# Compressing products after the whole fourth projection, and weight sums behind the last chunk's addition

## The chip, the cores and the metric

The kernel runs on one core of one Trainium2 chip. The metric is the device time of one execution in microseconds (us); the time before is the median of three runs, 2373.29 us.

## The reference, cut to what matters

Two layers of a decoder trunk run on one sequence of 512 tokens and 1024 features. Each layer has a gated feed-forward block, a mixing block and a second feed-forward block; the mixing block has three attention branches, one of which reads compressed keys and values.

```python
for l in range(DEPTH):                                     # DEPTH = 2
    h = rms_norm(x, ffn1_norm[l])
    x = x + 0.5 * swiglu(h, ffn1_w_gate[l], ffn1_w_up[l], ffn1_w_down[l])
    h = rms_norm(x, mix_norm[l])
    (nq, nkc, nvc, nks, nvs, nkw, nvw, ngate, sq, sk, sv, wq, wk, wv, bgate) = jnp.split(h @ w_in[l], SPLIT_POINTS, axis=-1)
    y_nsa = nsa_attention(...)             # compressed, selected and window branch
    y_sb = stick_breaking_attention(...)   # 4 heads
    y_swa = swa_sink_attention(...)
    merged = g0 * (y_nsa @ w_up_nsa[l]) + g1 * (y_sb @ w_up_sb[l]) + g2 * (y_swa @ w_up_swa[l])
    x = x + merged @ w_out[l]
    h = rms_norm(x, ffn2_norm[l])
    x = x + 0.5 * swiglu(h, ffn2_w_gate[l], ffn2_w_up[l], ffn2_w_down[l])

def compress(t, w1, w2):                   # t: keys or values, blocks of 32 tokens, step 16
    blocks = t[:, cmp_idx] + cmp_pos[:, None, :]
    blocks = blocks.transpose(0, 3, 1, 2, 4).reshape(B, G, n_cmp, CMP_LEN * Dh)
    return jax.nn.silu(blocks @ w1) @ w2   # w1: 2048 x 256, the "compressing products" are blocks @ w1
```

## The kernel before, in words

All data are 32-bit. A product is made of three: each operand is split into a high part (a cast to fp32r on ScalarE) and a low part (the difference, on VectorE), and TensorE adds high times high, high times low and low times high (`mm3`, lines 205 to 207). A weight block is fetched by SyncE into a raw tile (`fetch`, line 173, tag `wraw`, 3 buffers) and split into `whi` and `wlo` (`split`, lines 191 and 192, 3 buffers each). Tile, the framework, plans the order of the instructions on every engine itself: it walks the traced program with a simulated clock and takes, of what is ready, what was traced first. Buffers of one tag are handed out in the order in which they are asked for. Instructions made through `fpe`, `fact`, `fdve` keep the order of the program, and `behind(ins, earlier)` adds an edge that only fixes an order.

**The mixing block's front** (`mix_front`) makes six projections of the normed input (`project`, line 672 for the products). Each projection goes over four quarters of the input features; a quarter has one weight block and, at 512 columns, 24 products of 512 columns. Between projections stand pieces of the attention work: the generator `sb` gives the stick-breaking heads one half at a time (scores at lines 763 and 764, sigmoids on ScalarE at 832 and 833, a scan on VectorE at 838, transposes and the product with the values at 780 to 795), and `more` gives gate logits (24 products each, a 512 KB weight block), which fill TensorE where it would wait. The fourth projection of the change's name is index 4 of `GROUPS`, `nkv`, counted from zero. Its argument `mid` is called after each quarter g and traces the compressing products of the chunks in `COMPRESS[g]`: before, none after quarter 0, chunks 0 and 1 after quarter 1, chunk 2 after quarter 2, chunk 3 after quarter 3. A chunk (`compress_in`, products at line 939) has two weight blocks of 512 KB, one for keys and one for values, and 32 products of 256 columns, for which each block is split first. They add up in PSUM bank 2 (`bank("c")`), which the stick-breaking scores use until then (`bank("s")`).

**The feed-forward block** takes its gate and up products in a Strassen-like form: a `Pair` has seven products of 24 matmuls of 256 columns each (`product`, line 413 in the profile for all that keeps the program's order), made of four weight blocks a11, a12, a21, a22 and sums of them. s1 is a sum of two blocks made by DMA: SyncE loads the first (line 436), GpSimd's DMA adds the second into the same tile (line 437). s2 = s1 - a11, s3 and s4 are made on VectorE (line 442). The first three products of a pair are a11 with b11 (bank X), s1 with t1 (bank W) and s2 with t2 (bank X again, after a copy of X to Y on ScalarE). b and t are forms of the input x, made by `Crossed.add` chunk by chunk as x is finished (lines 279 to 342); the last chunk (k = 7) makes t2 at once and the rest late.

At the end of a block the first pair of the next is prepared ahead (`Pair.ahead`): `before_last` is called when the products of the last of the eight output chunks are traced and before its addition to x. There are three such places: from the mixing block to the second feed-forward block in both layers (addition at line 1225), and from the second feed-forward block of layer 0 to the first of layer 1 (line 648 makes half of the product, line 652 adds it). `ahead` loads the blocks, then traces a11's high and low part, s1's high part (446) and low part (450), the sum s2 (442) and s2's high part (446). Inside a feed-forward block `ahead` is used too, between its two phases and after the opening.

Of the kernel before, what the change touches and what calls it, by code (L numbers as in the profile page):

```python
# [23 lines left out]
KD = D // P  # L24
# [32 lines left out]

COMPRESS = ((), (0, 1), (2,), (3,))

# [37 lines left out]
def trunk(ctx, tc, I, out):  # L97
# [319 lines left out]
    class Pair:  # L417
# [21 lines left out]
        def sum(self, n, dve):  # L439
            a, b, op = self.SUMS[n]  # L440
            self.v[n] = whole("u")
            dve.tensor_tensor(self.v[n], self.v[a], self.v[b], op=op)

# [4 lines left out]
        def lo(self, n, dve):  # L448
            lo = wp.tile([P, 8, P], F32R, name=nm("wlo"), tag="wlo", bufs=3).rearrange("p a b -> p (a b)")
            dve.tensor_tensor(lo, self.v[n], f32(self.parts[n][0]), op=ALU.subtract)  # L450
            self.parts[n].append(lo)

        def product(self, o, n, form, first):
# [9 lines left out]

        def ahead(self):

            self.load("a11")
            self.load_sum()
            self.load("a12", "a21", "a22")
            self.hi("a11", act)
            self.lo("a11", dve)  # L470
            self.hi("s1", act)
            self.lo("s1", dve)
            self.sum("s2", dve)
            self.hi("s2", act)

        def gate(self, i, t):
# [115 lines left out]

    def ffn(l, which, nrm, after, before_last=lambda: None):
        gu_name, d_name = f"wgu{which}", f"wd{which}"
# [6 lines left out]
        for ph, ((f0, fn), cuts) in enumerate(PHASES):  # L601
# [30 lines left out]
            for d in range(KD):  # L632
# [18 lines left out]
                else:  # L651
                    dve.tensor_tensor(x[d], x[d], e, op=ALU.add)
                    after(d)


# [441 lines left out]

    def mix(l, nrm, nxt, before_last):
        early = iter(range(EARLY))
# [14 lines left out]
        psum(acc=(3, 7, 0, 1, 2, 4, 5, 6), f=(3, 7))  # L1114
        mix_back(l, nxt.add, gls, y_ns, y_sb, y_sw, before_last)

# [75 lines left out]

    def mix_back(l, after, gls, y_ns, y_sb, y_sw, before_last):

# [22 lines left out]
        for d in range(KD):  # L1217
# [5 lines left out]
            if d == KD - 1:  # L1223
                before_last()
            dve.tensor_tensor(x[d], p, x[d], op=ALU.add)
            after(d)


# [28 lines left out]
    for l in range(L):  # L1257
# [11 lines left out]
        def start(l, which, nxt):  # L1269
            nxt.first = Pair(l, f"wgu{which}", 0, nxt)  # L1270
            nxt.first.ahead()

        mix(l, nrm, nxt, lambda: start(l, 2, nxt))
        nrm = nxt
        if l + 1 < L:
            nxt = Crossed(3 * (l + 1))
            ffn(l, 2, nrm, nxt.add, lambda: start(l + 1, 1, nxt))
            nrm = nxt
# [67 lines left out]
```

## Time and profile before

| what | value |
|---|---|
| runs | 2368.54, 2373.29, 2373.84 us; median 2373.29 |
| profiled execution | 2371.2 us, its span on the engines 2369.4 us |
| TensorE busy | 2328.6 us, 98% of the span, 14484 products |
| VectorE busy | 1693.2 us, 71% |
| ScalarE busy | 1185.8 us, 50% |
| GpSimd busy | 478.4 us, 20% |
| DMA | 289 MB, 122 GB/s over the span |

A time in the profile counts from the span's start. Matmuls overlap, so the pace of a row of them is read from start to start. PEclk is the share of TensorE's full clock that was granted: 1.00 is 2.4 GHz, 0.50 is 1.2 GHz. What stands in brackets behind an instruction is the idle time of its engine before it and what ended that.

### The profile page before, as it was taken

How to read it: one execution, taken by the hardware profiler on the slowest of the kernel's cores; microseconds unless marked ns; L12 is line 12 of the kernel's file. 1: busy time of each engine (PE TensorE's matmuls, PEld its weight loads, DVE VectorE, ACT ScalarE, POOL GpSimd, SP SyncE). 2: the span in 40 equal slices, each digit the busy share in tenths (PEclk: the TensorE clock that was granted, in tenths of full speed). 3: DMA queues.
4: the chain of work that ended last, by engine and by line, in shares of the span. 5: the costliest groups of instructions: out<-in, count | busy, mean ns of one | idle time of the engine just before them, and what ended most of it. 6: DMA issues, size and time to landing. Idle time of an engine off the chain costs nothing. (4 is left out here: it accounts for less than half of the span.)

```text
span 2369.4 us, 37950 instructions
## 1 busy us (share of the span) xinstructions
PE 2328.6 (98%) x14484; PEld 2064.2 (87%) x14484; DVE 1693.2 (71%) x2979; ACT 1185.8 (50%) x2145; POOL 478.4 (20%) x617
## 2 busy tenths in 40 slices
PE   8999999999999999999999999999999999999999
PEld 8989987877888799899899899878778878998997
DVE  8855864776677798558788568638767777984684
ACT  6533543565666555335455345435556664552351
POOL 2011011523333510110100100114233344001100
PEclk9999999999999999999999999999999999999999
DMA  6534443232323345444344444422322233544433
GB/s 205 149 123 124 137 121 114 82 130 90 101 73 120 125 143 152 121 135 136 114 137 141 135 129 124 149 87 101 118 86 95 78 122 123 144 136 131 141 114 100
DMA packets 95474, 289.24 MB, mean 122 GB/s; under 512 B 11573, under 2 KB 13410, under 8 KB 95292
## 3 DMA queue, kind: packets, MB, share of 16 engines
q1 hardware_dynamic: 89100, 264.28, 33.6%
q0 software_dynamic: 6192, 22.55, 5.6%
q8 instruction: 113, 1.85, 0.3%
q14 instruction: 69, 0.57, 0.1%
HBM read 275.70 MB, written 11.08 MB: 121 GB/s over the span
## 5 line engine op out<-in xcount | busy, mean ns | idle before, releaser
L191 ACT CAST whi<-wraw 128x1024 fp32r<-128x1024 f32 (+4 forms) x224 | 193.1, 867 | 370.4 <-PE acc L207 244.4
L192 DVE TENSOR_TENSOR wlo<-wraw,whi 128x1024 fp32r<-128x1024 f32 (+4 forms) x224 | 239.7, 1075 | 180.0 <-ACT whi L191 179.9
L413 ACT CAST whi<-u 128x1024 fp32r<-128x1024 f32 x156 | 163.9, 1050 | 248.7 <-DVE u L413 160.1
L208 PE MATMUL acc<-u,wlo 128*128 128x512 f32 x704 | 275.9, 395 | 1.1 <-DVE wlo L192 1.1
L206 PE MATMUL acc<-u,whi 128*128 128x512 f32 x704 | 276.6, 395 | 0.0
L207 PE MATMUL acc<-u,whi 128*128 128x512 f32 x704 | 276.5, 394 | 0.0
L672 PE MATMUL acc<-whi,u 128*128 128x512 f32 (+2 forms) x768 | 220.4, 363 | 0.0
L413 DVE TENSOR_TENSOR wlo<-u,whi 128x1024 fp32r<-128x1024 f32 x164 | 204.4, 1246 | 20.9 <-ACT whi L413 20.4
L437 POOL DMA_DIRECT2D u<-in_wgu x43 | 37.7, 876 | 753.4 <-DMA u<-in_wgu 389.4
L413 PE MATMUL X<-u,whi 128*128 128x256 f32 x1376 | 181.4, 284 | 5.2 <-ACT Y L413 3.5
L413 PEld LDWEIGHTS X<-u,whi 128*128 128x128 f32 x1376 | 171.6, 190 | 8.9 <-ACT Y L413 3.9
L208 PEld LDWEIGHTS acc<-u,wlo 128*128 128x128 f32 x704 | 132.2, 188 | 32.9 <-DVE wlo L192 2.0
L206 PEld LDWEIGHTS acc<-u,whi 128*128 128x128 f32 x704 | 132.4, 188 | 31.6 <-ACT whi L191 0.8
L207 PEld LDWEIGHTS acc<-u,whi 128*128 128x128 f32 x704 | 132.3, 188 | 30.7
L672 PEld LDWEIGHTS acc<-whi,u 128*128 128x128 f32 x768 | 136.3, 188 | 23.4 <-issue 1.7
L672 PE MATMUL acc<-wlo,u 128*128 128x512 f32 (+2 forms) x384 | 138.6, 362 | 1.1 <-DVE wlo L192 1.1
L198 DVE TENSOR_TENSOR glo<-wraw,ghi 128x256 fp32r<-128x256 f32 x192 | 90.6, 473 | 54.4 <-ACT ghi L197 52.5
L197 ACT CAST ghi<-wraw 128x256 fp32r<-128x256 f32 x192 | 77.1, 403 | 103.3 <-PE acc L207 43.5
L238 POOL TENSOR_TENSOR ssum<-ssum,e 128x512 f32<-128x512 f32 x42 | 57.4, 1367 | 320.1 <-ACT e L237 313.3
L648 DVE SCALAR_TENSOR_TENSOR e<-acc,rrow 128x512 f32<-128x512 f32 x64 | 44.1, 690 | 108.6 <-PE acc L208 108.6
L206 PE MATMUL acc<-u,ghi 128*128 128x512 f32 x272 | 110.9, 408 | 0.7 <-ACT gates L1148 0.6
L208 PE MATMUL acc<-u,glo 128*128 128x512 f32 x272 | 109.1, 402 | 0.0
(330 smaller groups left out, 5797.6 us busy)
## 6 DMA issues: line engine op xcount, KB each, us to landing
wraw<-in_wgu SPq DMA_DIRECT2D x104, 512.0 KB, 4.3
tt<-in_wgu SPq DMA_DIRECT2D x68, 512.0 KB, 4.2
wraw<-in_wd SPq DMA_DIRECT2D x64, 384.0 KB, 3.1
wraw<-in_wbg SPq DMA_DIRECT2D x48, 512.0 KB, 3.7
u<-in_wgu SPq DMA_DIRECT2D x43, 512.0 KB, 4.6
u<-in_wgu POOLq DMA_DIRECT2D x43, 512.0 KB, 5.5
wraw<-in_wd SPq DMA_DIRECT2D x64, 320.0 KB, 3.1
wraw<-in_wup SPq DMA_DIRECT2D x16, 512.0 KB, 3.8
```

The lines of the kernel that those rows point to most:

```text
L191: marks["split"] = act.copy(hi, raw)
L192: dve.tensor_tensor(lo, raw, f32(hi), op=ALU.subtract)
L197: act.copy(hi, raw)
L198: dve.tensor_tensor(lo, raw, f32(hi), op=ALU.subtract)
L206: pe.matmul(o, w[0], a[0], start=start, stop=False)
L207: pe.matmul(o, w[0], a[1], start=False, stop=False)
L208: pe.matmul(o, w[1], a[0], start=False, stop=stop)
L238: pool.tensor_tensor(self.sum, self.sum, sq, op=ALU.add)
L413: return lambda *a, **kw: tc.keep_in_program_order(getattr(self.engine, op)(*a, **kw))
L437: pool.dma_start(self.v["s1"], I[self.name][self.l, self.f, 3], accum_op=ALU.add)
L648: dve.scalar_tensor_tensor(e, p, 0.5, nrm.row, ALU.mult, ALU.mult)
L672: pe.matmul(o, a, b[:, j], start=k + m + t % per == 0, stop=True, skip_group_check=True)
```

## The change

All compressing products are traced after the last quarter of the projection. `ahead` makes the sum s2 and s1's low part in a method of their own, `sums`, with s2 first; at the three places above it is called after the last chunk's addition and its forms, and both VectorE instructions get an order edge behind that addition. At the other calls of `ahead` only the order of the two is swapped.

```diff
-COMPRESS = ((), (0, 1), (2,), (3,))
+COMPRESS = ((), (), (), (0, 1, 2, 3))
...
-        def ahead(self):
+        def ahead(self, later=False):
 
             self.load("a11")
             self.load_sum()
             self.load("a12", "a21", "a22")
             self.hi("a11", act)
             self.lo("a11", dve)
             self.hi("s1", act)
-            self.lo("s1", dve)
-            self.sum("s2", dve)
+            if not later:
+                self.sums()
+
+        def sums(self, earlier=None):
+
+            made = [self.sum("s2", dve), self.lo("s1", dve)]
             self.hi("s2", act)
+            if earlier is not None:
+                for ins in made:
+                    behind(ins, earlier)
...
-    def ffn(l, which, nrm, after, before_last=lambda: None):
+    def ffn(l, which, nrm, after, before_last=lambda: None, behind_last=lambda ins: None):
...
                 else:
-                    dve.tensor_tensor(x[d], x[d], e, op=ALU.add)
+                    added = dve.tensor_tensor(x[d], x[d], e, op=ALU.add)
                     after(d)
+                    if d == KD - 1:
+                        behind_last(added)
...
             if d == KD - 1:
                 before_last()
-            dve.tensor_tensor(x[d], p, x[d], op=ALU.add)
+            added = dve.tensor_tensor(x[d], p, x[d], op=ALU.add)
             after(d)
+        behind_last(added)
...
         def start(l, which, nxt):
             nxt.first = Pair(l, f"wgu{which}", 0, nxt)
-            nxt.first.ahead()
+            nxt.first.ahead(True)
 
-        mix(l, nrm, nxt, lambda: start(l, 2, nxt))
+        mix(l, nrm, nxt, lambda: start(l, 2, nxt), lambda ins: nxt.first.sums(ins))
...
-            ffn(l, 2, nrm, nxt.add, lambda: start(l + 1, 1, nxt))
+            ffn(l, 2, nrm, nxt.add, lambda: start(l + 1, 1, nxt), lambda ins: nxt.first.sums(ins))
```

`Pair.sum` and `Pair.lo` now return their instruction, and `mix` and `mix_back` hand `behind_last` on.

## Rows read from the trace of the kernel before

**Rows 1.** Part 1 of the page: busy time, share of the span, instructions.
```profile
PE 2328.6 (98%) x14484; PEld 2064.2 (87%) x14484; DVE 1693.2 (71%) x2979; ACT 1185.8 (50%) x2145; POOL 478.4 (20%) x617
```

**Rows 2.** Busy time of each engine in four stretches, with granted clock.
```profile
core 0: us, PE busy (x) PEld busy (x) DVE busy (x) ACT busy (x) POOL busy (x), PEclk, DMA share, GB/s
...
491.00:504.50 13.50, 9.93 (x47) 7.29 (x45) 10.68 (x14) 9.83 (x22) 10.21 (x15) 0.75 0.12 39
...
508.60:526.00 17.40, 17.40 (x102) 15.10 (x100) 12.62 (x20) 9.71 (x17) 0.41 (x2) 1.00 0.64 211
...
1665.00:1678.50 13.50, 10.39 (x49) 7.95 (x48) 11.58 (x13) 9.95 (x22) 10.25 (x15) 0.75 0.11 40
...
1197.70:1204.50 6.80, 6.78 (x32) 6.78 (x33) 6.80 (x11) 2.98 (x5) 1.03 (x2) 0.52 0.76 192
```

**Rows 3.** Timeline of TensorE, layer 0, stick-breaking and the first compressing product.
```profile
498.11 0.47 PE L786 MATMUL t<-tri,e 128*128 128x128 f32 x1 [0.82 <-POOL e L839]
...
504.46 0.38 PE L939 MATMUL c<-whi,gl 128*128 128x256 f32 x1
```

**Rows 4.** Timeline of SyncE: loads of the chunks' and of the projection's weight blocks.
```profile
470.53 0.33 SPq L173 DMA_DIRECT2D wraw<-in_w1k  x1
...
488.03 0.33 SPq L173 DMA_DIRECT2D wraw<-in_wi_nkv  x1
...
509.15 0.33 SPq L173 DMA_DIRECT2D wraw<-in_wi_nkv  x1
```

**Rows 5.** Timeline of ScalarE: casts of weight blocks (L191) around the last score.
```profile
491.30 1.05 ACT L191 CAST whi<-wraw 128x1024 fp32r<-128x1024 f32 x1 [2.04 <-PE acc L672]
...
503.46 0.59 ACT L833 ACTIVATE e<-s 128x512 f32<-128x512 f32 x1
...
505.58 2.01 ACT L191 CAST whi<-wraw 128x1024 fp32r<-128x1024 f32 x2 [0.35 <-PE c L939]
```

**Rows 6.** Cast, difference and load of a weight block, 466 to 526 us.
```profile
L191 ACT CAST whi<-wraw 128x1024 fp32r<-128x1024 f32 x14 | 14.5, 1048 | 11.8 <-PE acc L672 5.9 <-DMA wraw<-in_wi_nkv 2.1 <-DMA wraw<-in_w1v 1.7
...
L192 DVE TENSOR_TENSOR wlo<-wraw,whi 128x1024 fp32r<-128x1024 f32 (+1 forms) x14 | 16.4, 1194 | 10.3 <-ACT whi L191 10.3
...
wraw<-in_w1k SPq DMA_DIRECT2D x4, 512.0 KB, 3.6
```

**Rows 7.** Timeline of TensorE from layer 0's second feed-forward block to layer 1.
```profile
1189.37 2.06 PE L413 MATMUL X<-u,whi 128*128 128x256 f32 x16
...
1194.11 1.11 PE L413 MATMUL W<-u,wlo 128*128 128x256 f32 x8
1197.72 1.86 PE L413 MATMUL X<-u,whi 128*128 128x256 f32 x7 [2.50 <-ACT Y L413]
...
1204.52 2.06 PE L413 MATMUL Y<-st,whi 128*128 128x256 f32 x16
```

**Rows 8.** Timeline of TensorE from the mixing to the feed-forward block, both layers.
```profile
844.89 2.06 PE L413 MATMUL X<-u,whi 128*128 128x256 f32 x16
...
851.58 0.95 PE L244 MATMUL f<-tri,ssum 128*128 128x1 f32 x8
...
855.23 2.06 PE L413 MATMUL Y<-st,whi 128*128 128x256 f32 x16
...
2020.46 2.06 PE L413 MATMUL X<-u,whi 128*128 128x256 f32 x16
...
2030.81 2.06 PE L413 MATMUL Y<-st,whi 128*128 128x256 f32 x16
```

**Rows 9.** Timeline of VectorE at the same place as rows 7.
```profile
1190.34 1.22 DVE L442 TENSOR_TENSOR u<-u,tt 128x1024 f32<-128x1024 f32 x1 [2.85 <-DMA u<-in_wgu]
...
1194.03 0.68 DVE L648 SCALAR_TENSOR_TENSOR e<-acc,rrow 128x512 f32<-128x512 f32 x1
1194.74 0.69 DVE L652 TENSOR_TENSOR gl<-gl,e 128x512 f32<-128x512 f32 x1
```

**Rows 10.** Timeline of ScalarE at the same place.
```profile
1197.09 0.57 ACT L413 COPY Y<-X 128x512 f32<-128x512 f32 x1
```

More of the change, by code (lines that the diff above doesn't have):

```diff
@@ L441, in sum @@
             self.v[n] = whole("u")
-            dve.tensor_tensor(self.v[n], self.v[a], self.v[b], op=op)
+            return dve.tensor_tensor(self.v[n], self.v[a], self.v[b], op=op)
         def hi(self, n, act):
@@ L449, in lo @@
             lo = wp.tile([P, 8, P], F32R, name=nm("wlo"), tag="wlo", bufs=3).rearrange("p a b -> p (a b)")
-            dve.tensor_tensor(lo, self.v[n], f32(self.parts[n][0]), op=ALU.subtract)
             self.parts[n].append(lo)
+            return dve.tensor_tensor(lo, self.v[n], f32(self.parts[n][0]), op=ALU.subtract)
         def product(self, o, n, form, first):
@@ L1096, in gate_logits, with mix @@
         return g
-    def mix(l, nrm, nxt, before_last):
+    def mix(l, nrm, nxt, before_last, behind_last):
         early = iter(range(EARLY))
@@ L1114, in mix @@
         psum(acc=(3, 7, 0, 1, 2, 4, 5, 6), f=(3, 7))
-        mix_back(l, nxt.add, gls, y_ns, y_sb, y_sw, before_last)
+        mix_back(l, nxt.add, gls, y_ns, y_sb, y_sw, before_last, behind_last)
     def mix_front(l, nrm, more):
@@ L1191, in mix_front, with mix_back @@
         return (nq, nk, nv, vc, gates), y_sb, y_sw
-    def mix_back(l, after, gls, y_ns, y_sb, y_sw, before_last):
+    def mix_back(l, after, gls, y_ns, y_sb, y_sw, before_last, behind_last):
         branches = [(br, k0, [split_y(y) for y in ys]) for br, k0, ys in ((1, 4, y_sb), (2, 6, y_sw), (0, 0, y_ns))]
```

## The prediction

> **What bounds the kernel now.** The busy times come first: TensorE is busy for 98% of the span and no other engine for more than 71% [rows 1]. So a change that leaves the products as they are can only win what TensorE loses between them, in idle time or at a lower clock. I looked for its gaps in the timeline and for the granted clock in stretches. Most losses lie in a few places; two of the kinds belong to the code that changes.
>
> The first is in the mixing block's front, once per layer. For 13.5 us TensorE has only stick-breaking work, waits for ScalarE and GpSimd between small pieces, and its clock falls: 9.93 us busy with 47 products at a mean clock of 0.75 in layer 0, 10.39 us with 49 in layer 1 [rows 2]; a typical wait is 0.82 us [rows 3]. The loads tell why nothing else fills it. The first chunk's block is asked for at 470.53, but the third quarter of the projection only at 488.03 and the fourth at 509.15 [rows 4]: they stand behind the chunks' blocks in the three raw and three split buffers. The third cast of a chunk's block is at 491.30, the next not before 505.58, and what ended that wait was a compressing product [rows 5]. In between all split buffers hold blocks of chunks 0 and 1, whose products cannot start, since their PSUM bank is that of the scores: the last sigmoid that reads a score starts at 503.46 [rows 5], the first compressing product at 504.46 [rows 3].
>
> The second is the hand-over to the next feed-forward block. From the first product of the new pair to the fourth, 72 matmuls, it takes 15.15 us after layer 0's second feed-forward block [rows 7], 10.34 and 10.35 after the mixing blocks [rows 8]. At the long one VectorE stands 2.85 us in the sum s2, for the DMA that makes s1; the last chunk's scaling runs only at 1194.03 and its addition at 1194.74 [rows 9], though its products ended before 1189.37, where the next pair begins [rows 7]. The copy of X to Y comes behind that chunk's forms on ScalarE, at 1197.09 [rows 10], and releases the next product after 2.50 us idle [rows 7]; then 6.8 us pass at a clock of 0.52 [rows 2].
>
> **The change part by part: the projection.** No instruction is added or removed; loads, splits and products of 8 blocks per layer change places with those of two quarters. Quarters three and four are now asked for before any chunk, so they are split as the first two leave the buffers, and their 48 products are ready when TensorE has nothing but stick-breaking. A 256-column product has a pace of 4.74 us / 40 = 0.118 us [rows 7], a 512-column one takes twice that, 0.24, so they are 11.4 us of work. What they can fill: the 47 instructions of the stretch, short and long ones, are at a mean of 0.118 us about 5.5 us of work, so 8.0 of the 13.5 us are lost in layer 0; the 49 of layer 1 give 7.7. With 11.4 us to fill in, all of that is covered and the clock has no reason to fall: 7.9 us per layer won, as an estimate. The ends are 5.7 us (layer 1's idle 3.1 plus half of the busy time, some 5.2 us, that ran at the lower level) and 8.4 us (the instructions at 0.11 us).
>
> What is given back: the chunks now come in one row. A block costs a load of 3.6 us, a cast of 1.05 and a difference of 1.19 [rows 6], and feeds only 8 x 0.118 = 0.95 us of products. When the last quarter's products end (call it E), two blocks can stand split and three more raw. Block 3 is split at E+2.3, blocks 4 and 5 each 1.2 later on VectorE; blocks 6 to 8 wait for a raw buffer, so block 6 is loaded at E+5.9 and split at E+8.1, block 8 is split at E+10.6 and used by E+11.6. The gate's block and the first block of the sixth projection wait in the same row: the former lands near E+11.7, the latter near E+13.0, split at E+15.3. From E to E+15.3 TensorE has 7.6 us of compressing products, some 2.4 us of the last stick-breaking head (eight products and as many transposes, counted in the timeline) and, from E+12.5, 2.8 us of the gate's 24 products: 2.5 us remain empty. VectorE was 12.62 us of 17.4 busy where this work stands now [rows 2] and gets the same work in less time, for which I add 1 us: 3.5 us given back. The ends are 0 (more transposes and norm work fill it, as they do around it now) and 7.7 us (nothing beside the chunks). I take 3.5 because no row shows TensorE quite without other work behind 508. Net 4.4 us per layer, 8.8 in all. SyncE's queue keeps its order otherwise: gate and sixth projection stay behind the chunks, as before.
>
> **The sums.** No work is added here either. At the long hand-over the last scaling can start when its products end, near 1189.5, addition at 1190.3, done at 1191.0; then t2's sum (0.5 us) and s2, whose DMA has landed at 1190.34, until 1192.6, s1's low part until 1193.8. That is needed at 1194.11 [rows 7], so it is in time by 0.3 us. Queued behind the moved sums on VectorE are only late forms and s3; who waits for s2 is its cast on ScalarE and, 3 us later, the third product. ScalarE does that chunk's forms, s2's cast and the copy to Y before about 1195.7; TensorE would ask at 1195.1. So the site becomes about as long as the other two: 15.15 - 10.35 = 4.8 us won, with ends of 0 and 5.7. The latter is against 72 x 0.118 + 0.95 = 9.45 us without a wait [rows 8]; 0 is the case that all small forms go first (some 3.4 us), s1's low part is 2.7 us late and the clock falls again. At the other two sites the same count shows 0.9 us of loss each; the addition comes 2.4 us earlier, I take 0.5 each, ends -1.0 and 0.9. Swapping s2 and s1's low part at the other calls costs nothing: the pair's products there lie several us behind both. Sum: 5.8 us.
>
> **Sum.** 8.8 + 5.8 = 14.6 us off the profiled execution's own 2371.2 us (2369.4 of span and 1.8 around it): 2356.6. That execution lies 2.1 us under the median of the runs shown, 2373.29, which is well inside their spread; I say 2357 us.
>
> **The rivals.** First, only the sums win. The chunks' row takes back all that the fill wins, 7.9 us, because its 7.7 us stay empty. For it: each block's split costs VectorE more (1.19) than its products cost TensorE (0.95). Against it: gate and stick-breaking products are there. 2373.3 - 5.8 = 2367.5, which I count as no change, since about 0.3% (7 us) is what a measurement of this kernel can tell.
>
> Second, only the projection wins: a new wait stands in the hand-over, s1's low part or the copy to Y a little late. 2373.3 - 8.8 = 2364.5. For it: the margin of 0.3 us. Against it: all of s1 and t2's inputs are there by 1191.
>
> Third, slower: the compressing products get their weights at VectorE's pace with that engine's other work between. If each difference drags 1 us of evacuation with it, a block needs 2.2 us; from block 3 on, block 8 is used at E+15.3 and, with a load of 4.6 us, the sixth projection starts at E+20. Of that 12.3 us are empty, and two falls of the clock in it cost about 3.4 us each (half of 6.8 [rows 2]): 19.1 us against 7.9 won, 11 per layer, 22 in all, less 5.8: 2389 us. It turns slower by over 0.3% when more than some 14 us per layer stay empty or at the lower clock. The Trainium skill warns of this shape (TensorE: Matmul & The Clock Gate, Loop structure matters more than you think): products that each wait for a DMA run with the clock down. By that rule alone the 64 products of a layer would take 15.2 us, not 7.6, and the forecast would be 2357 + 2 x 7.6 = 2372 us. The trace agrees so far that the clock does fall behind such waits [rows 2]. Against the rival: five of eight blocks are on chip in time.
>
> That the change does not do what it says: the planner, not the program, sets the order, and might still put the fourth quarter behind the scores; then the first rival's time holds, and it is counted there.
>
> **How the numbers follow.** The forecast gets 0.58, with a range of its own of 2350 to 2364 (ends of the fill and the give-back). The second rival gets 0.14, the first 0.17, the third 0.11. Faster: 0.58 + 0.14 = 0.72; same: 0.17; slower: 0.11. The range takes in the first two rivals and, below, the fill's upper end with nothing given back (2373.3 - 16.8 - 7.5 = 2349) and a few us of luck in the stages behind, which are planned anew: 2346 to 2369. Left out are the third rival and small tails.
>
> **What would show it.** Right: between the second quarter and the first compressing product TensorE is busy at clock 1.00 with 512-column products of the projection in both layers; four loads of the projection stand in a row on SyncE ahead of the first chunk's. Right for the sums: the long hand-over takes 10 to 11 us, at clock 1.00, and s2 comes behind the last addition on VectorE. Wrong: idle of more than 4 us per layer between compressing products, or between them and the sixth projection; a clock of 0.50 there; s1's low part ending behind the first 16 products of bank W. The forecast is also wrong if the sliding heads' stage, where TensorE waits for VectorE now, grows by what was won.

## The result and the profile after

The changed kernel takes 2387.85 us (median, 2386.19 to 2388.01) beside 2372.12 us for the kernel before (2368.54 to 2373.84): a ratio of 1.0068, with a 95% interval of 1.0056 to 1.0079. It is 15.7 us slower where 2357 us and a gain were forecast. The profiled execution has a span of 2386.2 us against 2369.4, so 16.8 us are to be found.

Part 1 of the page of the kernel after answers to [rows 1]. TensorE has the same instructions and 8.6 us more busy time: part of the loss is time at a lower clock, the rest is idle.

```profile
PE 2337.2 (98%) x14484; PEld 2074.2 (87%) x14484; DVE 1688.3 (71%) x2979; ACT 1183.9 (50%) x2145; POOL 484.5 (20%) x617
```

**Where it lies.** The next fence is TensorE's timeline of the kernel after at the three hand-overs; the first and the last line of each answer to [rows 7, 8].

```profile
847.16 0.51 PE L413 MATMUL X<-u,whi 128*128 128x256 f32 x3
...
857.46 1.01 PE L413 MATMUL X<-u,whi 128*128 128x256 f32 x3 [2.71 <-DVE u L316]
...
861.26 0.63 PE L413 MATMUL Y<-st,whi 128*128 128x256 f32 x2
...
1196.42 0.51 PE L413 MATMUL X<-u,whi 128*128 128x256 f32 x3
...
1203.78 0.62 PE L413 MATMUL W<-u,wlo 128*128 128x256 f32 x3 [2.45 <-DVE wlo L451]
...
1210.54 0.80 PE L413 MATMUL X<-u,whi 128*128 128x256 f32 x2 [2.04 <-DVE u L316]
...
1214.33 0.63 PE L413 MATMUL Y<-st,whi 128*128 128x256 f32 x2
...
2031.38 0.39 PE L413 MATMUL X<-u,whi 128*128 128x256 f32 x2
...
2045.48 0.63 PE L413 MATMUL Y<-st,whi 128*128 128x256 f32 x2
```

From the first product to the first of bank Y, the hand-overs take 14.10, 17.91 and 14.10 us where they took 10.34, 15.15 and 10.35 [rows 7, 8]. Cut at these marks, the 16.8 us are: 2.3 up to the first mark, 3.8 in the first hand-over, 1.0 until the long one, 2.8 in the long one, 1.1 until the third, 3.7 in the third and 2.1 behind it. So 10.3 us stand within the hand-overs that were to give 5.8, and another 3.1 in the stretches behind the first and the third, which hold the rest of the same pairs. The mixing fronts, which were to give 8.8, take 3.4 more.

**The stretches of the front.** Busy times and granted clock of the kernel after, columns as in [rows 2]; the first three and the last three rows are the fronts of the two layers, the three between them are hand-overs.

```profile
491.00:504.50 13.50, 13.50 (x72) 11.21 (x71) 8.63 (x14) 8.14 (x18) 8.05 (x9) 1.00 0.31 101
504.50:511.60 7.10, 5.36 (x27) 3.81 (x25) 7.03 (x18) 6.22 (x16) 3.28 (x6) 0.77 0.23 74
511.60:528.00 16.40, 13.47 (x83) 12.54 (x82) 14.52 (x26) 9.33 (x16) 6.11 (x9) 0.81 0.49 159
856.50:863.40 6.90, 5.94 (x28) 5.94 (x29) 5.32 (x15) 1.53 (x2) 0.00 (x0) 0.51 0.63 224
...
1204.50:1215.00 10.50, 8.46 (x41) 8.04 (x40) 10.23 (x23) 3.86 (x7) 1.22 (x2) 0.51 0.74 201
1672.00:1683.00 11.00, 11.00 (x60) 9.20 (x59) 6.14 (x8) 7.12 (x14) 4.13 (x5) 1.00 0.30 96
1683.00:1695.60 12.60, 10.77 (x55) 8.36 (x53) 12.24 (x26) 9.01 (x24) 7.71 (x12) 0.89 0.28 85
1695.60:1712.00 16.40, 12.48 (x83) 10.97 (x82) 14.48 (x26) 9.20 (x16) 5.97 (x9) 0.92 0.46 154
```

The stretch that was to be filled is filled: 13.50 of 13.50 us at a clock of 1.00, where it was 9.93 at 0.75 [rows 2]. What follows was full before (17.40 of 17.40 us at 1.00 [rows 2]) and now has 4.7 us empty and a mean clock of 0.77 to 0.81. Layer 1 shows the same, with 5.8 us empty. The gap has moved behind the fill.

The loads and the score chain of layer 0 after the change, lines of SyncE, TensorE, ScalarE and TensorE again, each engine in a fence of its own:

```profile
468.32 6.23 SPq L173 DMA_DIRECT2D wraw<-in_wi_nkv  x3
477.14 0.33 SPq L173 DMA_DIRECT2D wraw<-in_w1k  x1
```
```profile
509.24 0.80 PE L772 MATMUL s<-u,u 128*128 128x512 f32 x1 [0.56 <-ACT e L842]
...
511.69 0.54 PE L948 MATMUL c<-whi,gl 128*128 128x256 f32 x1
...
521.61 0.39 PE L948 MATMUL c<-whi,gl 128*128 128x256 f32 x1 [0.86 <-ACT whi L191]
...
524.62 0.44 PE L789 MATMUL o<-pt,u 128*128 128x384 f32 x1 [2.07 <-ACT pt L783]
```
```profile
511.00 0.59 ACT L842 ACTIVATE e<-s 128x512 f32<-128x512 f32 x1
...
520.51 1.04 ACT L191 CAST whi<-wraw 128x1024 fp32r<-128x1024 f32 x1 [2.13 <-DMA wraw<-in_w1k]
```

The projection's blocks are asked for in a row ahead of the chunks', as forecast. But the last head's chain of scores is late: the sigmoid that frees the compressing products' bank starts at 511.00 in place of 503.46 [rows 5], the first compressing product at 511.69 in place of 504.46 [rows 3]. Between 495 and 501 us TensorE now runs 23 projection products ahead of that head's first score, which starts at 500.66 where it started at 493.38 before. Then the compressing products, and what stands among them, wait: 0.86 us for the cast of a weight block, and 2.07 us for an instruction that stood behind two such casts on ScalarE, the first of which had waited 2.13 us for its load.

**The hand-overs.** VectorE of the kernel after, the first hand-over:

```profile
847.70 0.68 DVE L1234 TENSOR_TENSOR gl<-acc,gl 128x512 f32<-128x512 f32 x1
848.30 1.21 DVE L442 TENSOR_TENSOR u<-u,wraw 128x1024 f32<-128x1024 f32 x1
849.43 1.21 DVE L451 TENSOR_TENSOR wlo<-u,whi 128x1024 fp32r<-128x1024 f32 x1
850.57 1.52 DVE L279 SCALAR_TENSOR_TENSOR pt<-gl,norms,u 128x256 f32<-128x256 f32 x1
...
854.33 1.21 DVE L413 TENSOR_TENSOR wlo<-u,whi 128x1024 fp32r<-128x1024 f32 x1
...
855.86 1.21 DVE L413 TENSOR_TENSOR wlo<-wraw,whi 128x1024 fp32r<-128x1024 f32 x1
857.00 0.41 DVE L316 TENSOR_TENSOR u<-pt,u 128x256 fp32r<-128x256 f32 x1
```

The planner puts s2 and s1's low part, here called the sums, directly behind the addition, ahead of t2's form (L279). The form ends at 852.1, but its low part (L316) starts only at 857.00: among what VectorE does between are two more low parts of weight blocks (L413), s2's own and another, which in the kernel before came behind t2's low part (852.57, the two at 852.91 and 854.04). It ends at 857.4, and for that the product at 857.46 stood 2.71 us; the clock around and behind it is 0.51 (856.5 to 863.4 us).

The long hand-over: a line of ScalarE of the kernel before, then ScalarE and VectorE of the kernel after.

```profile
1190.42 1.05 ACT L446 CAST whi<-u 128x1024 fp32r<-128x1024 f32 x1 [2.88 <-DMA u<-in_wgu]
```
```profile
1197.98 1.05 ACT L446 CAST whi<-u 128x1024 fp32r<-128x1024 f32 x1 [3.35 <-DMA u<-in_wgu]
1198.93 0.40 ACT L315 CAST yn<-pt 128x256 fp32r<-128x256 f32 x1
```
```profile
1199.37 0.43 DVE L316 TENSOR_TENSOR yn<-pt,yn 128x256 fp32r<-128x256 f32 x1 [2.98 <-ACT yn L315]
...
1200.76 0.69 DVE L659 TENSOR_TENSOR gl<-gl,e 128x512 f32<-128x512 f32 x1
...
1202.51 1.22 DVE L451 TENSOR_TENSOR wlo<-u,whi 128x1024 fp32r<-128x1024 f32 x1
```

VectorE's own wait for s1's DMA [rows 9] is gone. But ScalarE's cast of s1 had waited 2.88 us for the same DMA in the kernel before already. It still does, 3.35 us, with form casts of the chunk before the last queued behind it, and VectorE waits 2.98 us for one of them. So the addition comes 4.3 us after the pair's first product (1200.76 - 1196.42), 1.0 us earlier than before (5.4 us, [rows 7, 9]), and the sums that were late before it are now late behind it.

### The profile page after: what moved, and what is told of

It is laid out like the page before. It is cut to its first block, busy times and chain, and to the rows that moved or that the text cites. A ratio compares the mean times of both kernels' runs of the same rounds, so it can differ in the third digit from the quotient of the medians.

```text
span 2386.2 us, 37947 instructions
## 1 busy us (share of the span) xinstructions
PE 2337.2 (98%) x14484; PEld 2074.2 (87%) x14484; DVE 1688.3 (71%) x2979; ACT 1183.9 (50%) x2145; POOL 484.5 (20%) x617
## 4 chain that ended last, share of the span: by engine, by line
PE 88%; DVE 7%; issue 2%; ACT 1%; DMA 1%; POOL 0%; SPq 0%; DVEq 0%; ACTq 0%
PE X L413 20%; PE acc L208 11%; PE acc L206 11%; PE acc L207 11%; PE W L413 10%; PE acc L681 8%; PE Y L413 5%; PE o L789 2%; PE s L772 1%; PE s L773 1%; PE f L747 1%; PE g L206 1%; PE g L207 1%; PE g L208 1%; PE t L795 1%
## 5 line engine op out<-in xcount | busy, mean ns | idle before, releaser
L191 ACT CAST whi<-wraw 128x1024 fp32r<-128x1024 f32 (+4 forms) x224 | 193.2, 866 | 373.6 <-PE acc L207 243.9
L413 ACT CAST whi<-u 128x1024 fp32r<-128x1024 f32 x156 | 163.8, 1050 | 256.1 <-DVE u L413 167.8
L413 DVE TENSOR_TENSOR wlo<-u,whi 128x1024 fp32r<-128x1024 f32 x164 | 204.5, 1247 | 22.0 <-ACT whi L413 21.6
L413 PE MATMUL X<-u,whi 128*128 128x256 f32 x1376 | 184.5, 287 | 9.1 <-DVE u L316 7.5
L413 PEld LDWEIGHTS X<-u,whi 128*128 128x128 f32 x1376 | 173.8, 192 | 12.2 <-DVE u L316 8.2
```

The costliest lines, as they stand in the source:

```text
L191: marks["split"] = act.copy(hi, raw)
L413: return lambda *a, **kw: tc.keep_in_program_order(getattr(self.engine, op)(*a, **kw))
```

## The experiments

Twelve more kernels ran. The table gives the ratio to the kernel before, run anew beside each (its medians lie between 2370.8 and 2372.1 us), with its interval and, from each profiled execution, the time in us of four parts: front 0 and front 1 (from the first product of a pair in bank X, 206.4 and 1383.2 us in the kernel before, to the first product of the block behind the mixing, so each holds the rest of a feed-forward block and the whole mixing block), and the first and the long hand-over as above. The third hand-over goes with the first.

| kernel | median us | ratio [interval] | front 0 | first hand-over | long hand-over | front 1 |
|---|---|---|---|---|---|---|
| before | 2372.12 | 1 | 638.5 | 10.3 | 15.2 | 637.3 |
| the change | 2387.85 | 1.0068 [1.0056, 1.0079] | 640.9 | 14.1 | 17.9 | 638.1 |
| compress_only | 2380.40 | 1.0042 [1.0027, 1.0057] | 643.5 | 10.4 | 15.0 | 639.3 |
| sums_only | 2382.14 | 1.0048 [1.0031, 1.0064] | 638.2 | 14.1 | 18.1 | 637.7 |
| sums_after_t2 | 2368.75 | 0.9988 [0.9979, 0.9997] | 638.2 | 10.4 | 15.7 | 633.1 |
| sums_after_t2_cast | 2364.43 | 0.9973 [0.9963, 0.9982] | 638.3 | 10.4 | 11.3 | 633.4 |
| compress_held | 2372.33 | 1.0003 [0.9993, 1.0013] | 638.4 | 10.4 | 15.4 | 635.9 |
| compress_half | 2377.33 | 1.0022 [1.0013, 1.0031] | 643.3 | 10.3 | 14.9 | 637.8 |
| compress_half_held | 2370.12 | 0.9993 [0.9984, 1.0003] | 636.3 | 10.4 | 14.4 | 634.9 |
| best_half_held | 2366.83 | 0.9983 [0.9974, 0.9992] | 637.9 | 10.1 | 12.5 | 633.7 |
| compress_once | 2356.40 | 0.9941 [0.9926, 0.9956] | 632.9 | 10.4 | 15.4 | 627.5 |
| held_once | 2357.16 | 0.9944 [0.9928, 0.9961] | 632.4 | 10.3 | 14.6 | 627.6 |
| after_mended | 2369.50 | 0.9992 [0.9983, 1.0002] | 640.8 | 10.4 | 11.7 | 637.4 |
| compress_loaded_once | 2377.68 | 1.0032 [1.0019, 1.0045] | 639.3 | 10.4 | 15.0 | 641.6 |

### The change in halves

**compress_only**: the kernel before with the new order of the compressing products alone.

```
-COMPRESS = ((), (0, 1), (2,), (3,))
+COMPRESS = ((), (), (), (0, 1, 2, 3))
```

> Only the compressing products move; the sums stay where they were. Aligning the two traces by the first product of each feed-forward block, the mixing fronts account for 2.4 us (layer 0) and 0.8 us (layer 1) of the 16.8 us that the profiled execution grew by. Theory A (two separate losses, most of it in the hand-overs): about 3 us above before, 2374 to 2377. Rival B (the third rival of the prediction: the compressing products without cover carry the whole loss): 2385 to 2390. In both, the last score of stick-breaking ends some 7 us later than before, because 23 products of the projection stand ahead of a score in TensorE's order.

Measured 2380.40 us. The hand-overs are those of the kernel before, the fronts 5.0 and 2.0 us longer. Neither range given was met: the time lies between the two.

**sums_only**: the changed kernel with the old order of the compressing products.

```
-COMPRESS = ((), (), (), (0, 1, 2, 3))
+COMPRESS = ((), (0, 1), (2,), (3,))
```

> Only the sums move; the compressing products stay where they were. Theory A: the three hand-overs take 4.8, 3.0 and 5.9 us more, 13.7 in all, 2384 to 2388; t2's low part comes behind s2's low part and another on VectorE, some 10 us after the pair's first product instead of 8, and the clock falls to 0.50 in all three. Rival B: the sums win what was forecast or nothing, 2366 to 2373.

Measured 2382.14 us, 2 us under theory A's range and far over B's. The fronts are those of the kernel before within 0.4 us, the hand-overs 14.1 and 18.1 us, as in the whole change within 0.2 us. So each half loses alone, in its own stage: 9.2 and 10.9 us against the kernel before in those runs (2371.25). Together that would be 20 us, 4 more than the whole change lost; where the 4 us went wasn't followed.

### The sums

**sums_after_t2**: sums_only, with the order of VectorE set by edges: s1's low part behind t2's form, s2 behind that, s2's own low part behind t2's low part.

```
-            made = [self.sum("s2", dve), self.lo("s1", dve)]
+            made = [self.lo("s1", dve), self.sum("s2", dve)]
...
-                for ins in made:
-                    behind(ins, earlier)
+                behind(made[0], marks["t2"])
+                behind(made[1], made[0])
...
-        p.lo("s2", fdve)
+        low = p.lo("s2", fdve)
+        if first and "t2 low" in marks:
+            behind(low, marks["t2 low"])
```

> As sums_only, but VectorE takes the last chunk's t2 form first, then s1's low part, then s2, and t2's low part ahead of s2's low part. Theory A (what costs is that the sums stand ahead of t2's forms): the two hand-overs after the mixing block return to 10.3 to 11.3 us at clock 1.00; the long one stays at 15 to 17.5 us, since its last scaling waits behind forms whose casts stand behind s1's cast on ScalarE; total 2371 to 2376. Rival C (it is the late start of the sums as such, not what they stand ahead of): the two stay above 14 us, total 2382 to 2388.

Measured 2368.75 us, under theory A's range. The first and third hand-over are back at 10.4 us, without a clock fall, as A has it; C falls. The run sets two orders at once, the sums behind t2's form and t2's low part ahead of s2's, so it does not tell what each of the two is worth. TensorE and ScalarE of this kernel at the long one:

```profile
1195.78 1.21 PE L413 MATMUL W<-u,wlo 128*128 128x256 f32 x8 [1.93 <-DVE wlo L451]
...
1199.65 0.58 PE L413 MATMUL X<-u,whi 128*128 128x256 f32 x1 [1.26 <-ACT Y L413]
```
```profile
1190.59 1.05 ACT L446 CAST whi<-u 128x1024 fp32r<-128x1024 f32 x1 [3.53 <-DMA u<-in_wgu]
```

There the cast still waits for the DMA, so the long hand-over keeps its 15.7 us.

**sums_after_t2_cast**: the same, with that cast put behind the form casts (L315) that were queued behind it on ScalarE.

```
-            self.hi("s1", act)
-            if not later:
+            cast = self.hi("s1", act)
+            if later:
+                behind(cast, marks["form cast"])
+            else:
                 self.sums()
```

> As sums_after_t2, and s1's cast on ScalarE comes behind the casts of the chunk before the last. Theory A (at the long hand-over the wait for s1's DMA only moved from VectorE's sum to ScalarE's cast, with the forms behind it): the last addition there ends within 3 us of the pair's first product instead of 5, the hand-over takes 10.5 to 12.5 us at clock 1.00, total 2366 to 2371. Rival C: as sums_after_t2, within 1 us.

Measured 2364.43 us, 1.6 us under theory A's range, 4.3 us less than without the cast's edge, and 0.27% less than the kernel before: the lowest time of the study among kernels that leave no work out. The wait for s1 is still 2.70 us long on ScalarE, but nothing that VectorE needs stands behind it. TensorE of this kernel at the long hand-over, which has one wait of over 0.5 us left; and its row of the view by stretches for 1197.2 to 1204.7 us, where the kernel before had a clock of 0.52 [rows 2]:

```profile
1196.97 1.10 PE L413 MATMUL X<-u,whi 128*128 128x256 f32 x7 [1.08 <-ACT Y L413]
```
```profile
1197.20:1204.70 7.50, 7.19 (x59) 6.97 (x59) 7.50 (x13) 5.32 (x8) 0.00 (x0) 1.00 0.78 242
```

11.3 us against 15.2. About half of the gain is luck: front 1 is 4.2 and 3.9 us shorter in these two kernels. The kernel before has a wait of 3.08 us at 1755 us, where the sliding heads' products wait for VectorE; these two have no wait over 1.1 us at that place. Nothing in the edges aims at it; the planner's order of that stage came out otherwise, and in sums_only, with no more than the sums moved, TensorE waits 3.30 us there.

### The projection: is it the late chain, or the pace of the weights?

Two theories for the loss in the front. A: the 23 products ahead of the last head's first score delay its chain (each score's sigmoids, scan and products, one behind the other), and all that waits for it, by 7 us. B: 64 compressing products in a row run at the pace at which their weights get ready.

**compress_held**: compress_only, with edges that put the products of quarters 3 and 4 behind scores, twelve at a time.

```
+HELD = {(2, 0): (2, 3), (2, 1): (2, 3), (2, 2): (3, 0), (2, 3): (3, 0), (3, 0): (3, 1), (3, 1): (3, 1), (3, 2): (3, 2), (3, 3): (3, 2)}
...
-                    pe.matmul(o, a, b[:, j], start=k + m + t % per == 0, stop=True, skip_group_check=True)
+                    made = pe.matmul(o, a, b[:, j], start=k + m + t % per == 0, stop=True, skip_group_check=True)
+                    if (g, t) in held:
+                        behind(made, chain[held[g, t]])
```

> The kernel before with the new order of the compressing products alone (all behind the fourth quarter), and order edges on TensorE that spread the 48 projection products of quarters 3 and 4 over the score chain of the last head: twelve of them behind the score before the chain, twelve each behind the chain's first, second and third score. Theory A (the half lost because 23 products stood ahead of the last head's first score, so that its chain and all that waits for it came 7 us later): the chain ends at 502 to 506 again, the first compressing product starts before 507, the lost time behind it falls from 9.7 us to under 4 us in the first layer, and the time is 2364 to 2372 us. Rival B (the half lost because 64 compressing products without projection products among them run at the pace at which their weights come): the chain is early again, but the compressing stretch keeps waits on the weights' low parts of over 5 us in the first layer, and the time is 2373 to 2381 us.

Measured 2372.33 us, between the two. The edges give back 8 us of the 9, but the time is that of the kernel before. The last head's last score comes at 506.6 and not at 510.0, the first compressing product at 509.6. Neither theory's signs are met: 5.1 us are lost behind the chain where A has under 4, and by name TensorE waits 0.7 us for low parts where B has over 5.

**compress_half**: the kernel before with `COMPRESS = ((), (), (0, 1), (2, 3))`.

> The kernel before with two weight blocks' compressing products behind the third quarter and two behind the fourth, no edges. Both theories: the planner lets the chain run as in the kernel before with few products in it, so 6 to 8 us stay lost beside the scores in each layer, and quarter 4 covers the second pair of blocks. Theory A and rival B alike: 2368 to 2376 us. It is the base of the next run.

Measured 2377.33 us, above what was expected: the chain ends 4 us late here too (last score at 505.8, before at 501.7) and front 0 is 4.8 us longer.

**compress_half_held**: the same two and two, with quarter 3's products held behind scores, six at a time.

```
+HELD = {(2, 0): (2, 3), (2, 1): (3, 0), (2, 2): (3, 1), (2, 3): (3, 2)}
```

> The same two and two, with quarter 3's 24 products spread over the last head's score chain by order edges, six behind each score. Theory A: the chain is not delayed by over 2 us and the fill is kept: 3 to 5 us less in each layer than in the kernel before, 2361 to 2367 us. Rival B: 2361 to 2369 us too, and faster than the run with all four blocks at the end, by 6 us or more, because quarter 4 stands among the compressing products; by theory A the two differ by under 5 us.

Measured 2370.12 us, not to be told from the kernel before, though its profiled execution has 2.2 and 2.4 us less in the fronts. The chain is early (last score 500.6); it did not bring the 3 to 5 us per layer. With 2.2 us to compress_held it meets A's condition and not B's, but the time of neither theory is met.

**best_half_held**: compress_half_held and sums_after_t2_cast together.

```
-COMPRESS = ((), (0, 1), (2,), (3,))
+COMPRESS = ((), (), (0, 1), (2, 3))
+HELD = {(2, 0): (2, 3), (2, 1): (3, 0), (2, 2): (3, 1), (2, 3): (3, 2)}
```

> The last one together with the sums behind t2's form and the cast behind the last chunk's casts, which alone gave 0.9973 of the kernel before (6.5 us less). If the two parts add, as their stretches are apart: 2354 to 2361 us. If one spoils the other (another shift of the stages behind): 2362 to 2368 us.

This cut is against sums_after_t2_cast. Measured 2366.83 us, in the second range: the parts do not add. The mended sums alone are at 0.9973 against 0.9983; the intervals overlap, so this kernel is at least no better.

**compress_once**: compress_only, but the first chunk's weight block of keys and that of values are loaded, cast and split and used for all four chunks; the other three chunks' blocks are left out. So it prices that work and is no version to use, and neither are held_once and compress_loaded_once, which use the first chunk's blocks for all four too.

```
-            w = load(f"w1{which}", (l, c), 4, CW)
+            if c == 0:
+                held_w[which] = load(f"w1{which}", (l, c), 4, CW)
+            w = held_w[which]
```

> The run with the new order of the compressing products alone, but the weights of the compressing products are loaded, cast and split once for each of keys and values and used for all four blocks (six of eight loads, casts and low parts left out, the products all there). Theory A (the half lost through the last head's delayed chain alone): the chain comes as late as with all the loads, and 2374 to 2380 us stay. Rival B (the pace of the weights through three raw and three split buffers alone): the waits in the compressing stretch go, and the time is 2362 to 2369 us. If both take part: 2369 to 2374 us.

Measured 2356.40 us, 24 us less than compress_only and below all three of the ranges. The chain is even later in this kernel (its last score at 513.6, the first compressing product at 515.9), and it costs nothing: A alone falls. The fronts are 5.6 and 9.8 us shorter than in the kernel before.

**held_once**: the same with the edges of compress_held.

```
+HELD = {(2, 0): (2, 3), (2, 1): (2, 3), (2, 2): (3, 0), (2, 3): (3, 0), (3, 0): (3, 1), (3, 1): (3, 1), (3, 2): (3, 2), (3, 3): (3, 2)}
```

> The run with the products spread over the score chain by order edges, again with the compressing weights loaded once. With the chain early and the weights there, what stays lost between 500 and 530 us should fall from 8.8 to under 4 us in the first layer, and the time to 2358 to 2366 us, which is the gain that the filled score chain was worth (8 us a layer were lost beside it before). If it stays at 2370 us or more, neither the chain nor the weights are what took the gain back.

Measured 2357.16 us, 0.8 us under the range: with the weights there, an early chain is worth nothing more.

**compress_loaded_once**: compress_once took away loads, casts and low parts at once. Here only six of eight loads go.

```
-            w = load(f"w1{which}", (l, c), 4, CW)
+            if c == 0:
+                held_w[which] = fetch(f"w1{which}", (l, c), 4, CW)
+            w = split(held_w[which], 4, CW)
```

> The run with the new order of the compressing products alone, but each of the two weight blocks is loaded once and its cast and its low part are made anew for each of the four blocks: six of eight loads left out, all casts and low parts there. It parts what the run with weights loaded, cast and split once took away together. If the transfers and the three raw buffers that they wait for set the pace (ScalarE's cast stood 4.0 us for a transfer at 517 to 521 us): 2356 to 2364 us, close to the run with everything once, with no wait over 0.6 us in the compressing stretch. If the casts, the low parts (VectorE is 98% busy there, low part 1.2 us each) or the split buffers set it: 2371 us or more, with the waits on low parts and casts there as before. If both take part: 2364 to 2371 us.

Measured 2377.68 us, as the case of the casts, low parts or split buffers has it: without six of eight transfers most of the loss stays. The next rows are all of the stretch 500 to 525 us of layer 0, columns as in [rows 2], for the kernel before, compress_only, compress_held, compress_once and compress_loaded_once in this order.

```profile
500.00:525.00 25.00, 24.47 (x142) 21.51 (x142) 18.40 (x27) 14.86 (x25) 4.63 (x11) 0.91 0.45 148
```
```profile
500.00:525.00 25.00, 19.96 (x116) 16.37 (x115) 24.33 (x48) 16.57 (x34) 9.80 (x14) 0.93 0.33 105
```
```profile
500.00:525.00 25.00, 21.05 (x132) 17.25 (x131) 23.49 (x50) 18.35 (x36) 5.05 (x11) 1.00 0.44 146
```
```profile
500.00:525.00 25.00, 24.58 (x159) 21.54 (x158) 20.63 (x44) 14.31 (x32) 13.87 (x17) 1.00 0.21 64
```
```profile
500.00:525.00 25.00, 19.56 (x122) 15.42 (x120) 24.59 (x48) 17.91 (x36) 11.29 (x17) 1.00 0.07 21
```

VectorE is the full engine: 24.33 and 24.59 of 25 us where TensorE has 5 us empty, 20.63 where TensorE is full; in the kernel before it had 18.40. ScalarE is never over 18.35, and in the last row the transfers move next to nothing (21 GB/s). Some of TensorE's waits name it too, in the timeline of compress_loaded_once:

```profile
516.59 0.39 PE L943 MATMUL c<-wlo,gl 128*128 128x256 f32 x1 [0.84 <-DVE wlo L192]
...
525.24 0.38 PE L943 MATMUL c<-wlo,gl 128*128 128x256 f32 x1 [0.81 <-DVE wlo L192]
```

So VectorE's queue is the likely limit. In these 25 us it makes seven low parts of weight blocks in the kernel before and in compress_only alike (8.3 and 9.4 us in all). New there are two more of the last head's scans and the projection's own evacuations and norm steps, which the early quarters have brought forward. compress_held helps because the scans come earlier and fewer of them stand among the low parts; it does not remove a low part.

What is shown and what is argued: compress_once shows that the loss hangs on the making of the weights, and compress_loaded_once that most of it is not the transfers. That it is VectorE, and not ScalarE's casts or the three split buffers, is argued from the busy times; no run left out the low parts alone. TensorE's own waits do not settle it: of 6.0 us between 500 and 535 us in compress_only 4.2 are for ScalarE and 1.2 for VectorE. One of ScalarE's leads back to VectorE: a cast waited 4.00 us for a block whose load was issued at 517.75, just behind the end of a low part at 517.72.

Where the time goes can be counted from each trace as TensorE's lost time: its idle time and half of the time that it was busy at a clock of 0.50. Each cell has layer 0 and layer 1 in us; the stretches are 480 to 505.5, to 537 and to 609 us in layer 0, and the same 1174.2 us later in layer 1, shifted with the front's start in each kernel.

| kernel | beside the scores | the row of compressing products | the next stages |
|---|---|---|---|
| before | 6.5, 6.3 | 0.0, 0.0 | 5.0, 6.9 |
| the change | 0.3, 0.4 | 9.7, 8.8 | 5.4, 5.6 |
| compress_only | 0.1, 0.4 | 9.5, 9.2 | 7.0, 5.7 |
| compress_held | 0.0, 0.0 | 5.1, 5.0 | 5.7, 5.7 |
| compress_half_held | 0.8, 0.8 | 2.8, 2.8 | 7.3, 8.5 |
| compress_loaded_once | 0.2, 0.0 | 5.5, 10.1 | 5.0, 7.0 |
| compress_once | 0.0, 0.3 | 0.4, 0.1 | 7.5, 4.6 |
| sums_after_t2_cast | 6.3, 6.6 | 0.0, 0.2 | 5.3, 3.2 |
| after_mended | 0.0, 0.0 | 6.6, 6.7 | 7.1, 5.5 |

The fill wins some 6 us per layer in every kernel that moves the products. In compress_only and the change the row behind it takes 9 to 10 us back. With the chain early (compress_held) the two together win 1.4 and 1.3 us, and with half of the chunks behind quarter 3 (compress_half_held) 2.9 and 2.7. What the next stages lose moves by several us from kernel to kernel, and that hides such a gain.

A second wait for VectorE stands in these next stages. VectorE and TensorE of compress_only:

```profile
583.59 4.66 DVE L709 TENSOR_TENSOR rw<-rw,hr 128x512 f32<-128x512 f32 x4
588.17 1.48 DVE L198 TENSOR_TENSOR glo<-wraw,ghi 128x256 fp32r<-128x256 f32 x1
```
```profile
589.70 0.50 PE L208 MATMUL g<-u,glo 128*128 128x512 f32 x1 [3.04 <-DVE glo L198]
```

A low part that TensorE needs stands behind four norm multiplications, in both layers of compress_only, compress_held, after_mended and the whole change, 3.0 us long (0.78 us in layer 0 of the kernel before), and the granted clock falls to 0.50 behind it, from 590.8 to 597.7 us in compress_only. It wasn't tried alone.

**after_mended**: the whole change with all three mends (sums behind t2's form, cast behind the form casts, products held behind scores).

```
-COMPRESS = ((), (0, 1), (2,), (3,))
+COMPRESS = ((), (), (), (0, 1, 2, 3))
+HELD = {(2, 0): (2, 3), (2, 1): (2, 3), (2, 2): (3, 0), (2, 3): (3, 0), (3, 0): (3, 1), (3, 1): (3, 1), (3, 2): (3, 2), (3, 3): (3, 2)}
```

This diff is against sums_after_t2_cast; the edges themselves are those of compress_held.

> The whole change with both mends: the order edges that spread the projection products over the score chain, the sums ordered behind t2's form, the first sum's cast behind the last chunk's casts. If these three are all that made the change slower, the hand-overs are 10.4, 10.4 to 11.5 and 10.4 us and the time is that of the kernel with the mended sums and little more or less: 2361 to 2368 us. If something else in the change costs, over 2372 us.

Measured 2369.50 us, between the two. The hand-overs are as expected (10.4, 11.7 and 10.4 us). The fronts are 2.5 and 4.0 us longer than in sums_after_t2_cast, which keeps the old order of the compressing products. By the table of lost time the row behind the fill takes back just what the fill wins (6.6 and 6.7 us against 6.3 and 6.6); the rest is lost in the next stages, 1.8 and 2.3 us. The version to keep is sums_after_t2_cast.

## Why the prediction was wrong, step by step

- **What bounds the kernel, and the fill.** The mechanism was right: the empty stretch beside the scores was the place, the loads moved as told, and TensorE is full there at 1.00. The size was somewhat high: 7.9 us per layer were forecast, with ends of 5.7 and 8.4; lost there in the kernel before were 6.5 and 6.3 us, and compress_once wins 6.5 and 6.0 of them. Its fronts are 5.6 and 9.8 us shorter, 15.4 in all, which is near 2 x 7.9 by luck: its next stages lose 2.5 us more in layer 0 and 2.3 less in layer 1.
- **What is given back.** This term failed. It was set at 3.5 us per layer, with ends of 0 and 7.7. In compress_only the row of compressing products loses 9.5 and 9.2 us, where nothing was lost before: more than the fill wins, and outside the ends. The next stages add 2.0 us in layer 0 and lose 1.2 less in layer 1, which makes up the 5.0 and 2.0 us by which the fronts grew; the prediction named a growth there as a sign of being wrong but priced it at nothing. The working counted loads, buffers and the low parts one after another, and "for which I add 1 us" for the rest of VectorE's work. That engine is 24.33 of 25 us busy there. The row that should have warned is the 12.62 of 17.4 us [rows 2]: it was 73% busy with that work already, and the same work had to fit into less time together with the projection's evacuations. That this 1 us is the part that was too small is argued, as said above; that the term as a whole was, is measured.
- **The score chain** was not priced at all. That products put into a gap are also put ahead of the chain that made the gap was left out. By itself it costs nothing (compress_once); together with the making of the weights it costs 8 us, as compress_held against compress_only shows.
- **The clock.** The forecast had it at 1.00 once the gap was filled. It holds in the filled stretch; behind it the mean is 0.77 to 0.81 in layer 0 and 0.89 to 0.92 in layer 1.
- **The sums.** The step that failed is the order on VectorE: "then t2's sum (0.5 us) and s2". The planner puts s2 and s1's low part ahead of t2's form, because the edge asks only that they follow the addition, and two more low parts ahead of t2's low part. "Queued behind the moved sums on VectorE are only late forms and s3" was wrong: t2's form and its low part were. Where a gain of 0.5 us each was forecast at the two short hand-overs, with ends of -1.0 and 0.9, 3.75 us each were lost: TensorE waits 2.71 us for t2's low part, and the clock falls, which the bound did not hold. With the orders set by edges (sums_after_t2) both are back at 10.4 us.
- **The long hand-over.** That "the last scaling can start when its products end" failed: VectorE's wait for s1 was taken away, but ScalarE's cast waits for the same DMA, as its 2.88 us in the kernel before show, and the prediction did not follow that. With both orders set the hand-over takes 11.3 us, so 3.8 of the 4.8 us forecast were there to win: the mechanism was right, the edge to reach it was not the one in the change.
- **The rivals.** The third one named the mechanism of the front ("the compressing products get their weights at VectorE's pace with that engine's other work between") and, by the time alone, lay at 2389 us next to the measured 2387.85. That nearness is luck: it had 11 us lost in each layer and 5.8 won at the hand-overs; measured were 5.0 and 2.0 us lost in the fronts of compress_only and 10.9 us lost with the sums alone. Its falls of the clock did come, two in each layer's row of compress_only. The first two rivals each took one half as won; neither was. The rule of the Trainium skill (TensorE: Matmul & The Clock Gate, Loop structure matters more than you think) is about products that each stand behind a long wait for a DMA. Here no such case arose: the wait of [rows 7] that the prediction set beside it was for ScalarE's copy, and the row of compressing products of layer 0 ran with shorter waits, at 1.00 in compress_held and compress_loaded_once and at 0.77 to 0.81 in the change.
- **What stays open.** Whether a fourth raw or split buffer would help wasn't tried, and no run relieved VectorE alone. compress_half_held was only joined with the mended sums, and its next stages were not mended, though it loses 3.6 us per layer beside the scores and in the row together, where the kernel before loses 6.5 and 6.3. Why the two halves together cost 4 us less than their sum wasn't followed.

## What to carry to other kernels

Work put into an engine's gap moves the neighbours' work with it: before filling TensorE's gap, count what the engines that feed it (here VectorE) must then do in the next stretch, all of it, against its length. An order edge that says only "behind this" lets the planner run the moved work at once, ahead of what the same result was wanted for; name what has to come first. And before a wait for a DMA is taken from one engine's queue, look in the trace for every other engine that waits for the same data: here ScalarE's cast did already.

## What the runs showed of the hardware that was not expected

Some of VectorE's instructions take longer when they start while GpSimd runs. t2's form (128x256) takes 0.48 us in the kernel before, with GpSimd idle at all three of its places, and 1.52 us in the kernel after, beside this instruction of GpSimd:

```profile
849.59 2.21 POOL L238 TENSOR_TENSOR ssum<-ssum,e 128x512 f32<-128x512 f32 x1 [3.10 <-ACT e L237]
```

s1's low part, which had started 0.16 us before that instruction (849.43), takes 1.21 us as ever, and GpSimd's instruction 2.21 us where it takes 1.28 us in the kernel before. The sum s2 takes 1.22 us with GpSimd idle and 2.31 us beside the same line of GpSimd (in sums_after_t2). The four norm multiplications of the fence further above take 4.66 us beside GpSimd's L711, a tensor_tensor, and 2.71 us in the kernel before beside its L878, a tensor_scalar: not every instruction of GpSimd does it. The second that t2's form lost was lost in the kernel before too, by the form behind it (L310, 1.55 us at 849.57). So moving an instruction on VectorE can change its length, or another's, by 1 us, which no count of durations from one place shows.

The granted clock did not go by the length of single waits. It fell to 0.50 at 856.5 us, within the wait of 2.71 us of the first hand-over, and stayed there for 6.8 us. In the front of the change it fell at 508.4 us, also for 6.8 us, with no wait over 0.6 us in the 20 us before. And in compress_held four waits of 0.3 to 1.3 us within 7 us left it at 1.00.
